# Delta-rule heads of a hybrid encoder layer: spacing, PSUM banks, evictions and tables changed together

## The chip, the core and the metric

The kernel is one launch on one core of a Trainium2 chip. The core has a matrix engine (TensorE, PE in the rows; its weight loads are PEld), VectorE (DVE), ScalarE (ACT), GpSimd (POOL) and a queue that issues transfers (SyncE, SP). The metric is the device time of the launch in microseconds, and lower is better.

## The reference

One encoder layer is applied to 256 prompt tokens and 512 sample tokens (T = 768 together), width 2048, and then normed. The layer projects to 12 groups of columns; a gated delta rule in both directions (8 heads of 128, chunks of 64) and a latent attention (8 heads) run on them; both are gated, projected, mixed and projected again.

```python
proj = rmsnorm(x, norm_in) @ w_in
(qkv, gate_a, a_f, a_b, b_f, b_b, q_lat, kv_lat, k_rope, gate_b, gm_a, gm_b) = split(proj)
qkv = silu(depthwise_conv(qkv)); q_a, k_a = l2norm(q), l2norm(k)      # per head
# gated_delta_chunked, per head and chunk i, forward, and backward on flipped tokens:
a = strict_lower(k_beta @ k.T * decay) + I
u, w = solve_unit_lower(a, [v * beta, k_beta * exp(gc)])
v_new = u - w @ S
o     = (q * exp(g)) @ S + attn @ v_new
S     = S * exp(g_last) + k_dec.T @ v_new
o_a = rmsnorm(o_fwd + o_bwd) * silu(gate_a)
o_b = latent_attention(rmsnorm(q_lat) @ w_q_b, rmsnorm(kv_lat) @ w_kv_b) * silu(gate_b)
m = sigmoid(gm_a) * (o_a @ w_pa) + sigmoid(gm_b) * (o_b @ w_pb)
y = rmsnorm(x + m @ w_out)
```

The kernel puts two chunks of 64 tokens into one tile of 128, so a head has 6 tiles: one sequence of 4 (the sample) and one of 2 (the prompt).

## The kernel before

Products are done in float32 precision from high and low halves, three matmuls each (`project`, L467 on; the weights are cut into halves by `weights`: ScalarE casts `whi`, GpSimd or VectorE subtracts for `wlo`). In time the program has five stages: `w_in` by seven products of half-size blocks (0 to 1236 us); nine more projections of `OTHERS` columns with a sigmoid each, and then the kn, v, qr and qn projections of phase 2 (to 1835); attention beside the `w_pa` projections (to 2110); `w_pb` and `w_out` by seven products again.

The heads of the delta rule (`gdn`, L592 on) are tasks whose matmuls are laid between those of the projections of the second stage. The order on TensorE is the order in which the program is built: every matmul adds its planned cost to `self.clock` (`pin`), a task that yields w comes back when the clock has moved by w, and a matmul is tied to the one before it by a no-sync dependency. `WAIT` is the space between the links of a chain, `STEP` that between pieces of the substitution, `PACE` that between heads. The other engines' order is left to a scheduler, except where `here_on` pins an instruction to the place on its engine at which it was written.

Per head: `gdn_decays` builds E from `rh` (a product of mask and gate, on GpSimd) by two matmuls and an Exp; `gdn_front` transposes k and q, keeps `ktok`, and forms U, the strictly lower blocks; `gdn_values` makes the norms of q and k and `vs`; `gdn_blocks` inverts the 32x32 diagonal blocks by 31 steps of two VectorE operations (L736, L738); `gdn_place` spreads the blocks into X and W, eight copies on ScalarE (L754) and VectorE transposes (L757); `gdn_merge`, one per direction, makes the 64- and 128-wide inverses by 32x32 and 64x64 matmuls; then four chains `gdn_chain` (two sequences, two directions) carry the state S from tile to tile, each tile in three links: S against k and q, r against X (which gives `vn`), `vn` against k and E; `gdn_end` adds the directions, norms, gates and stores the head to `oa_d`.

All small matmuls of the heads and all of attention write to `aps`, tiles of one PSUM bank from a pool of four (`apsum`). In attention the scores of a 128-token block are three matmuls of the 128 unrotated dimensions, one of `qpe` with `kpe[0]` on all 128 rows, and one of `qpe` with `kpe[1]` on 64 rows.

Of the kernel before, what the change touches and what calls it, by code (L numbers as in the profile page):

```python
# [28 lines left out]
WAIT = 2300.0  # L29
STEP = 2500.0  # L30
PACE = 46000.0
# [23 lines left out]
class Layer:  # L55
# [72 lines left out]
    def apsum(self):  # L128
        return self.aux.tile([P, 512], F32, name="aps", tag="a")
# [38 lines left out]
    def work_pools(self):  # L168

        self.les = ExitStack()  # L170
        self.ev = self.pool("ev")
        self.pes = ExitStack()
        self.main = self.pool("main", 2, PSUM, self.pes)
        self.aux = self.pool("aux", 4, PSUM, self.pes)
# [343 lines left out]
    def gates(self):  # L518
# [24 lines left out]
        nc.scalar.activation(u, u, AF.Ln)  # L543
# [14 lines left out]
        nc.scalar.activation(ex, cv, AF.Exp)  # L558
# [20 lines left out]
    def gdn_setup(self):  # L579
        nc, gp = self.nc, self.gp  # L580
        self.X = [gp.tile([P, NCH, P], F32, name=f"X{d}") for d in range(2)]
        self.W = [gp.tile([P, NCH, 64], F32, name=f"W{d}") for d in range(2)]
        for t in self.X + self.W:
            nc.gpsimd.memset(t, 0.0)
# [51 lines left out]
    def gdn_decays(self, s):  # L636
# [3 lines left out]
        for d in range(2):  # L640
            mask = self.minc[d].unsqueeze(1).broadcast_to([P, 3, P])
            for g0 in (0, 3):
                parts = []
                for src in (self.ghi, self.glo):
                    rh = gp.tile([P, 3, P], F32R, name="rh", tag="rh", bufs=3)
                    nc.gpsimd.tensor_tensor(rh, mask, src[:, g0:g0 + 3, d * 8 + h].bitcast(F32).unsqueeze(2).broadcast_to([P, 3, P]), op=ALU.mult)
                    parts.append(rh)
                yield 4000
# [6 lines left out]
        yield 3500  # L655
        s["decayed"] = True

    def gdn_front(self, s):
# [5 lines left out]
        for c0, n, ps in self.tposed(kT):  # L664
            nc.vector.tensor_copy(ktok[:, c0:c0 + n, :], ps)
# [12 lines left out]
        U = s["U"] = gp.tile([P, 2, NCH, P], F32, name="U", bufs=2)  # L678
# [14 lines left out]
    def gdn_values(self, s):  # L693
# [21 lines left out]
    def gdn_blocks(self, s):  # L715
# [3 lines left out]
        U, X, W, V = s["U"], self.X, self.W, self.V  # L719
# [25 lines left out]
    def gdn_place(self, s, R):  # L745

        nc, X, W = self.nc, self.X, self.W
        cols = [R[:, :, 0:24].rearrange("p a (g d n) -> p d n a g", g=2, d=2)[:, d] for d in range(2)]
        for b in range(4):
# [3 lines left out]
            for d, t in zip((1, 0), dst):  # L753
                nc.scalar.copy(t.rearrange("p n (a g) -> p n a g", g=2), cols[d][r])  # L754
# [4 lines left out]
    def gdn_merge(self, s, d):  # L759

        nc, gp, U, X, W = self.nc, self.gp, s["U"][:, d], self.X[d], self.W[d]
# [12 lines left out]
        yield 2600  # L774
# [7 lines left out]
        for p in range(2):  # L782
            A, B = src(p), dst(p)
            nc.vector.tensor_scalar(X[A, :, B], x1[A, :192].rearrange("p (n c) -> p n c", c=32), -1.0, None, op0=ALU.mult)
            if p == d:
                nc.vector.tensor_scalar(W[B, :, wc], x1[B, 192:384].rearrange("p (n c) -> p n c", c=32), -1.0, None, op0=ALU.mult)
        yield 2600
# [5 lines left out]
        nc.vector.tensor_copy(q2s[B], q2[B, :384].rearrange("p (n c) -> p n c", c=64))  # L793
        yield 2600
# [3 lines left out]
        nc.vector.tensor_scalar(X[A, :, B], x2[A, :384].rearrange("p (n c) -> p n c", c=64), -1.0, None, op0=ALU.mult)  # L798
# [6 lines left out]
    def gdn_chain(self, s, q, d):  # L805
# [3 lines left out]
        for step, n in enumerate(chunks):  # L809
# [4 lines left out]
            else:  # L814
                p1 = self.apsum()
                self.mm(p1[:, 0:P], s["kq"][:, 0, ts], S, start=True, stop=True)
                self.mm(p1[:, P:2 * P], s["kq"][:, 1, ts], S, start=True, stop=True)
                r = gp.tile([P, P], F32, name=f"r{q}{d}", tag=f"r{q}{d}")
                nc.vector.scalar_tensor_tensor(r, p1[:, 0:P], self.eg[:, d, n, h:h + 1], s["vs"][:, n, :], op0=ALU.mult, op1=ALU.subtract)
                t = gp.tile([P, P], F32, name=f"t{q}{d}", tag=f"t{q}{d}")  # L820
                nc.scalar.mul(t, p1[:, P:2 * P], self.eg[:, d, n, h:h + 1])
# [9 lines left out]
            p3 = self.apsum()  # L831
# [710 lines left out]
```

## Time and profile before

| what | value |
|---|---|
| time, median of 3 runs (lowest, highest) | 2544.79 us (2543.53, 2544.82) |
| time of the profiled execution | 2548.74 us |
| its span in the profile | 2547.0 us |
| TensorE busy in the span | 2430.3 us (95%) |
| VectorE, ScalarE, GpSimd busy | 1960.1, 1112.6, 539.1 us |

The span runs from the first to the last instruction that the profile shows; 1.74 us of the execution's time lie around it. Busy times are sums of an engine's instructions, overlaps counted once. The rows further down name a tile by the program's name for it, with "out<-in", and a line of the program as L and its number.

### The profile page before, as it was taken

What the parts mean: (1) busy time and instruction counts of PE and PEld (TensorE: products, weight loads), DVE (VectorE), ACT (ScalarE), POOL (GpSimd) and SP (SyncE); (2) the same over time, 40 slices, a digit from 0 to 9 for tenths busy, and PEclk for the clock granted to TensorE, in tenths of its full rate; (3) what the DMA queues carried; (4) which work ended last, traced back from release to release, by engine and by line L of the source; (5) the groups of instructions that cost most, each with busy time, mean ns of one, the idle gap of its engine ahead of it and who ended that gap; (6) DMA issues with size and microseconds to landing.
All of it is one profiled execution on the core that took longest, in us unless ns stands there. A gap on an engine that the chain in (4) does not pass through costs nothing. (4 is left out here: it accounts for less than half of the span.)

```text
span 2547.0 us, 41374 instructions
## 1 busy us (share of the span) xinstructions
PE 2430.3 (95%) x15062; PEld 2303.9 (90%) x15062; DVE 1960.1 (77%) x4294; ACT 1112.6 (44%) x2337; POOL 539.1 (21%) x456
## 2 busy tenths in 40 slices
PE   7999999999999999999989999989999999979997
PEld 6999999999999999999978878878888788968997
DVE  8777888888888887777458899888344567988876
ACT  6553343333333343334526665444344543334442
POOL 5210000000000000000734444443443331032112
PEclk9999999999999999999979999999999999989998
DMA  5542223233222232223312253322375444533346
GB/s 178 180 159 85 102 96 105 97 108 103 97 98 98 96 118 98 98 98 119 125 46 78 77 175 127 119 87 82 114 234 172 137 159 148 176 102 123 130 161 217
DMA packets 157564, 313.45 MB, mean 123 GB/s; under 512 B 17072, under 2 KB 35888, under 8 KB 157360
## 3 DMA queue, kind: packets, MB, share of 16 engines
q1 hardware_dynamic: 157360, 310.81, 36.8%
q8 instruction: 118, 1.93, 0.3%
q14 instruction: 86, 0.70, 0.1%
HBM read 236.33 MB, written 72.45 MB: 121 GB/s over the span
## 5 line engine op out<-in xcount | busy, mean ns | idle before, releaser
L198 ACT CAST Thi<-T 128x512 fp32r<-128x512 f32 x400 | 247.5, 619 | 660.2 <-PE P L86 286.7
L200 DVE TENSOR_TENSOR Tlo<-T,Thi 128x512 fp32r<-128x512 f32 x400 | 284.1, 710 | 225.8 <-ACT Thi L198 221.9
L458 POOL TENSOR_TENSOR wlo<-wraw,whi 128x512 fp32r<-128x512 f32 x113 | 154.3, 1367 | 1179.2 <-ACT whi L453 1124.0
L194 DVE TENSOR_TENSOR T<-wraw,T 128x128 f32<-128x128 f32 x800 | 261.1, 327 | 14.0
L199 DVE TENSOR_TENSOR wlo<-wraw,whi 128x384 fp32r<-128x384 f32 x400 | 227.1, 568 | 0.3 <-ACT whi L191 0.2
L191 ACT CAST whi<-wraw 128x384 fp32r<-128x384 f32 x400 | 203.2, 508 | 39.0 <-PE P L86 31.1
L194 DVE TENSOR_TENSOR T<-wraw 128x256 f32<-128x256 f32 x400 | 169.5, 424 | 9.3 <-DMA wraw<-in_w_pb 6.7
L453 ACT CAST whi<-wraw 128x512 fp32r<-128x512 f32 x130 | 79.9, 617 | 108.5 <-PE ps L86 87.9
L573 DVE SCALAR_TENSOR_TENSOR f<-pad,cols,f 128x772 f32<-128x772 f32 x96 | 97.2, 1012 | 0.1
L736 DVE TENSOR_TENSOR spare<-Y,V 128x126 f32<-128x126 f32 (+22 forms) x248 | 92.0, 371 | 4.8
L738 DVE TENSOR_TENSOR Y<-Y,spare 128x126 f32<-128x126 f32 (+22 forms) x248 | 88.7, 358 | 4.7
L86 PE MATMUL ps<-ch,wlo 128*128 128x512 f32 (+1 forms) x288 | 79.0, 353 | 0.0
L86 PE MATMUL ps<-cl,whi 128*128 128x512 f32 (+1 forms) x288 | 78.7, 351 | 0.0
L86 PE MATMUL ps<-ch,whi 128*128 128x512 f32 (+1 forms) x288 | 78.4, 351 | 0.0
L86 PE MATMUL P<-mS,Thi 128*128 128x384 f32 x224 | 76.4, 343 | 0.7 <-ACT s L230 0.6
L86 PE MATMUL ps<-oah,whi 128*128 128x512 f32 (+1 forms) x256 | 68.4, 345 | 1.6 <-DVE g L1198 1.6
L896 POOL TENSOR_TENSOR acc<-acc,f 128x768 f32<-128x768 f32 x13 | 24.9, 1917 | 206.0 <-DVE wlo L199 131.7
L86 PE MATMUL ps<-oal,whi 128*128 128x512 f32 (+1 forms) x256 | 68.2, 345 | 0.0
L86 PE MATMUL ps<-oah,wlo 128*128 128x512 f32 (+1 forms) x256 | 68.0, 345 | 0.0
L223 DVE TENSOR_TENSOR f<-P,f 128x384 f32<-128x384 f32 x117 | 64.1, 549 | 0.2
L1296 POOL TENSOR_TENSOR rstd<-rstd,x 128x768 f32<-128x768 f32 x13 | 32.8, 2523 | 138.3 <-ACT x L1295 137.9
L1438 POOL TENSOR_TENSOR mX<-R,mH 128x768 fp32r<-128x768 f32 x8 | 30.3, 3782 | 133.0 <-ACT mH L1439 115.5
(779 smaller groups left out, 8158.9 us busy)
## 6 DMA issues: line engine op xcount, KB each, us to landing
wraw<-in_w_in SPq DMA_DIRECT2D x356, 256.0 KB, 2.7
wraw<-in_w_out SPq DMA_DIRECT2D x64, 256.0 KB, 2.7
wraw<-in_w_pa SPq DMA_DIRECT2D x32, 256.0 KB, 3.5
wraw<-in_w_pb SPq DMA_DIRECT2D x32, 256.0 KB, 3.8
xa<-in_xT SPq DMA_DIRECT2D x16, 384.0 KB, 3.7
xtok<-in_x SPq DMA_DIRECT2D x24, 256.0 KB, 3.7
qkv_d<-f SPq DMA_DIRECT2D x24, 256.0 KB, 2.0
sma_d<-f SPq DMA_DIRECT2D x16, 384.0 KB, 2.5
```

Source lines behind the costliest of these rows:

```text
L86: ins = self.nc.tensor.matmul(out, lhsT, rhs, start=start, stop=stop, **kw)
L191: nc.scalar.copy(hi[:, 1:], raw[:, 1:])
L194: tt = lambda o, x, y: self.after_floor(nc.vector.tensor_tensor(o, x, y, op=ALU.add))
L198: nc.scalar.copy(thi, t)
L199: first = nc.vector.tensor_tensor(lo[:, 1:], raw[:, 1:], hi[:, 1:].bitcast(F32), op=ALU.subtract)
L200: last = nc.vector.tensor_tensor(tlo, t, thi.bitcast(F32), op=ALU.subtract)
L223: add = lambda out, a, b, op=ALU.add: nc.vector.tensor_tensor(out, a, b, op=op)
L453: copy = nc.scalar.copy(hi, raw)
L458: eng.tensor_tensor(lo, raw, hi.bitcast(F32), op=ALU.subtract)
L573: nc.vector.scalar_tensor_tensor(acc, pad[:, k:k + 772], w[:, ct, k:k + 1], acc, op0=ALU.mult, op1=ALU.add)
L736: nc.vector.tensor_tensor(tmp[:, :a, :w], Y[:, :a, j:j + 1].broadcast_to([P, a, w]), V[:, j:j + 1, j + 1:].broadcast_to([P, a, w]), op=ALU ...
L738: nc.vector.tensor_tensor(Y[:, :a, j + 1:], Y[:, :a, j + 1:], tmp[:, :a, :w], op=ALU.subtract)
```

## The change

1. **Spaces.** `WAIT` 2300 to 3000, `STEP` 2500 to 2700, `PACE` 46000 to 51000, the spaces inside `gdn_merge` 2600 to 2900, those of `gdn_decays` 4000 to 3000 for head 0 and 9000 for the others.
2. **PSUM.** `aps` has two banks while the heads run. A new pool `link` holds one bank per direction; the two chains of a direction use its two halves. When the heads are done that pool is closed and `aps` gets two more banks.
3. **Inverses.** Two sets of X, taken in turn; a head is placed once the head before the last has finished its chains. U has one buffer instead of two and waits until the head before is merged.
4. **Evictions** of `ktok`, of the merges' X, W and `q2s`, of `vn` and of the first S go from VectorE to ScalarE.
5. **Tables.** The set with both Ln and Exp is loaded once; Sqrt and reciprocal of `gdn_values` and `gdn_end` become Ln, Exp and one Newton step of small GpSimd operations (`inverse_root`); the nine sigmoids of `OTHERS` move to the third stage (`mixed`). The ScalarE copies of `gdn_place` and the Ln of the gates are pinned with `here_on`.
6. **Small moves.** The zeroing of X and W goes from GpSimd to VectorE, and so does `rh` of head 0.
7. **Scores.** The matmul of `qpe` with `kpe[1]` runs on all 128 rows.

```diff
-WAIT = 2300.0
-STEP = 2500.0
-PACE = 46000.0
+WAIT = 3000.0
+STEP = 2700.0
+PACE = 51000.0
...
     def apsum(self):
-        return self.aux.tile([P, 512], F32, name="aps", tag="a")
+        self.aux.append(self.aux.pop(0))
+        return self.aux[-1].tile([P, 512], F32, name="aps", tag="a")
...
-        self.aux = self.pool("aux", 4, PSUM, self.pes)
+        self.cps = ExitStack()
+        self.aux = [self.pool("aux", 2, PSUM, self.pes)]
+        self.link = self.pool("link", 1, PSUM, self.cps)
...
+        both = nc.scalar.preload_act_table_set("natural_log_exp_and_others")
+        self.here_on(both)
...
-        while s["prev"] and not s["prev"].get("chained"):
+        while s["h"] > 1 and not s["prev"]["prev"].get("chained"):
             yield 300
         self.gdn_place(s, R)
...
-                    nc.gpsimd.tensor_tensor(rh, mask, ...)
+                    (nc.gpsimd if h else nc.vector).tensor_tensor(rh, mask, ...)
                     parts.append(rh)
-                yield 4000
+                yield 3000 if h == 0 else 9000
...
-            nc.vector.tensor_copy(ktok[:, c0:c0 + n, :], ps)
+            nc.scalar.copy(ktok[:, c0:c0 + n, :], ps)
...
-        U = s["U"] = gp.tile([P, 2, NCH, P], F32, name="U", bufs=2)
+        while h and s["prev"]["merged"] < 2:
+            yield 500
+        U = s["U"] = gp.tile([P, 2, NCH, P], F32, name="U")
...
-        nc.scalar.activation(sk, ss, AF.Sqrt, bias=self.eps)
-        s["rq"] = small("rq", [NCH])
-        nc.vector.reciprocal(s["rq"], sk[:, 1, :])
+        rr = small("rr", [2, NCH])
+        nc.gpsimd.tensor_scalar(ss, ss, EPS, None, op0=ALU.add)
+        self.inverse_root(rr, ss, sk)
+        s["rq"] = rr[:, 1]
+        nc.gpsimd.tensor_tensor(sk[:, 0], ss[:, 0], rr[:, 0], op=ALU.mult)
...
-                nc.scalar.copy(t.rearrange("p n (a g) -> p n a g", g=2), cols[d][r])
+                self.here_on(nc.scalar.copy(t.rearrange("p n (a g) -> p n a g", g=2), cols[d][r]))
...
-        nc.vector.tensor_copy(q2s[B], q2[B, :384].rearrange("p (n c) -> p n c", c=64))
-        yield 2600
+        nc.scalar.copy(q2s[B], q2[B, :384].rearrange("p (n c) -> p n c", c=64))
+        yield 2900
...
+        bank = self.link.tile([P, 2, 256], F32, name=f"link{d}")
         for q in range(2):
-            self.spawn(self.gdn_chain(s, q, d), WAIT)
+            self.spawn(self.gdn_chain(s, q, d, bank[:, q]), WAIT)
...
-            p2 = self.apsum()
-            self.mm(p2[:, 0:P], self.X[d][:, n, :], r, start=True, stop=True)
+            self.mm(ps[:, 0:P], self.X[h % 2][d][:, n, :], r, start=True, stop=True)
             vn = gp.tile([P, P], F32, name=f"vn{q}{d}", tag=f"r{q}{d}")
-            nc.vector.tensor_scalar(vn, p2[:, 0:P], s["cc" if first else "ncc"][:, d, n:n + 1], None, op0=ALU.mult)
+            nc.scalar.mul(vn, ps[:, 0:P], s["cc" if first else "ncc"][:, d, n:n + 1])
...
+    def inverse_root(self, y, x, t):
+        nc = self.nc
+        nc.scalar.activation(y, x, AF.Ln)
+        nc.scalar.activation(y, y, AF.Exp, scale=-0.5)
+        nc.gpsimd.tensor_tensor(t, y, y, op=ALU.mult)
+        nc.gpsimd.tensor_tensor(t, t, x, op=ALU.mult)
+        nc.gpsimd.tensor_scalar(t, t, -0.5, 1.5, op0=ALU.mult, op1=ALU.add)
+        nc.gpsimd.tensor_tensor(y, y, t, op=ALU.mult)
...
             ps = yield from self.project(KT, self.xs)
             f = self.evt()
             self.scaled(f, ps)
-            nc.scalar.activation(f, f, AF.Sigmoid)
...
-                self.mm(s, qpe[h][:64, qs], kpe[1][:64, keys], start=False, stop=True)
+                self.mm(s, qpe[h][:, qs], kpe[1][:, keys], start=False, stop=True)
...
                 x = raws[j][i]
+                if 72 + j + 8 * i in OTHERS:
+                    nc.scalar.activation(g, g, AF.Sigmoid)
```

Up to the decays of the first head, at the end of the first stage, the order on TensorE is the same in both kernels. The next rows are ScalarE's order, first of before and then of the change, at the placing of head 0 (`spare` holds the inverted blocks, E are decays of later heads, `whi` the weights of the running projection).

```order
L653 ACT_TABLE_LOAD
L653 ACTIVATE E<-aps 128x384
L453 CAST whi<-wraw 128x512
L653 ACTIVATE E<-aps 128x384
L754 COPY X_12973<-spare 32x6x32
L754 COPY W_12974<-spare 32x6x32
L754 COPY X_12973<-spare 32x6x32
L453 CAST whi<-wraw 128x512
L754 COPY W_12974<-spare 32x6x32
L754 COPY X_12973<-spare 32x6x32
```

```order
L661 ACTIVATE E<-aps 128x384
L456 CAST whi<-wraw 128x512 x2
L661 ACTIVATE E<-aps 128x384
L456 CAST whi<-wraw 128x512
L766 COPY X_12977<-spare 32x6x32
L766 COPY W_12980<-spare 32x6x32
L766 COPY X_12977<-spare 32x6x32
L766 COPY W_12980<-spare 32x6x32
L766 COPY X_12977<-spare 32x6x32
L766 COPY W_12980<-spare 32x6x32
```

The table load is gone, three casts of weights stand beside the last two decays' Exp where one stood, and the cast that stood among the copies is behind them. On TensorE 184 matmuls of the projection now stand between the last product of U of head 0 and its first merge (`aps<-W,U`), where 162 stood. The following rows are TensorE's order at the first links of head 0's chains, before and then changed (`vs` against X starts a chain, `ps` are the projection's matmuls; what a row waits for stands in brackets, "Activation" for ScalarE).

```order
L86 MATMUL aps<-vs,X_12973 128x128 [waits DVE_49,Activation_49]
L86 MATMUL aps<-vs,X_12973 128x128 [waits PE_49]
L86 MATMUL aps<-vs,X_12972 128x128 [waits PE_49]
L86 MATMUL aps<-vs,X_12972 128x128 [waits Activation_49]
L86 MATMUL aps<-kq 128x256 [waits DVE_49]
L86 MATMUL aps<-kq 128x256
L86 MATMUL ps<-B5l,whi 128x384 x2
L86 MATMUL ps<-B5h,wlo 128x384 x2
L86 MATMUL ps<-B6h,whi 128x384 x2
L86 MATMUL aps<-vn_13927,kd_13929 128x128 [waits DVE_49]
```

```order
L86 MATMUL link_13869<-vs,X_12977 128x128
L86 MATMUL aps<-rh,mr 128x384 [waits PE_49,Activation_49]
L86 MATMUL aps<-rh,mr 128x384 [waits Pool_49]
L86 MATMUL link_13882<-vs,X_12976 128x128
L86 MATMUL link_13869<-vs,X_12977 128x128 [waits Activation_49]
L86 MATMUL ps<-B5l,whi 128x384 x2
L86 MATMUL ps<-B5h,wlo 128x384
L86 MATMUL link_13882<-vs,X_12976 128x128 [waits Activation_49]
L86 MATMUL ps<-B5h,wlo 128x384
L86 MATMUL ps<-B6h,whi 128x384 x2
L86 MATMUL aps<-kq 128x256 [waits PE_49]
L86 MATMUL link_13869<-vn_13915,kd_13917 128x128 [waits Activation_49]
```

The two sequences of a direction stood side by side, each in a bank of its own; now the second writes to the half beside the first's (`link_13869` twice), and waits until ScalarE has read the first. The last rows are VectorE's order before and ScalarE's now, for the `vn` and S of the same links.

```order
L826 TENSOR_SCALAR vn_13939<-aps,cc 128x128
L826 TENSOR_SCALAR vn_13945<-aps,cc 128x128
L686 SCALAR_TENSOR_TENSOR U<-aps,cc,E 128x128 x4
L729 STREAM_TRANSPOSE PK<-U 32x2x192
L838 COPY S_13969<-aps 128x128
```

```order
L456 CAST whi<-wraw 128x512
L698 COPY qk<-aps 128x256
L838 ACTIVATE vn_13915<-link_13869,cc 128x128
L661 ACTIVATE E<-aps 128x384
L838 ACTIVATE vn_13934<-link_13882,cc 128x128
L838 ACTIVATE vn_13920<-link_13869,cc 128x128
L698 COPY qk<-aps 128x256
L838 ACTIVATE vn_13939<-link_13882,cc 128x128
```

`vn` stood between blocks of U on VectorE, and now stands behind casts of weights and copies of `qk` on ScalarE.

The transposes of the last head's output stand 138 matmuls of projections ahead of the third stage's first one before, and 78 now; the number of projection matmuls from one head to the next is about 187 in both.

## Rows read from the trace of the kernel before

**Rows 1.** The page's first part: busy us, share, instructions.

```profile
PE 2430.3 (95%) x15062; PEld 2303.9 (90%) x15062; DVE 1960.1 (77%) x4294; ACT 1112.6 (44%) x2337; POOL 539.1 (21%) x456
```

**Rows 2.** Windows by stage: length, then busy PE, PEld, DVE, ACT, POOL; granted clock.

```profile
1286.00:1340.00 54.00, 43.49 (x303) 38.12 (x304) 27.40 (x84) 17.84 (x45) 12.34 (x14) 0.65 0.10 33
1340.00:1835.00 495.00, 460.10 (x3736) 407.32 (x3735) 400.31 (x1054) 261.34 (x722) 209.85 (x234) 0.97 0.33 108
1835.00:2110.00 275.00, 274.08 (x1568) 225.55 (x1567) 148.50 (x304) 132.74 (x271) 104.03 (x64) 1.00 0.53 173
2110.00:2547.00 437.00, 389.04 (x2218) 377.64 (x2216) 358.75 (x691) 165.92 (x302) 89.90 (x43) 0.94 0.46 150
```

**Rows 3.** TensorE's waits from 1236 to 1835: us, times, longest.

```profile
PE aps L86 <- POOL rh L646: 9.7, 1, 9.7
PE aps L86 <- ACT t L821: 8.2, 7, 2.2
```

**Rows 4.** Windows of the stretches at half clock: the first, and the sum of all five.

```profile
1295.18:1332.73 37.55, 30.95 (x223) 25.98 (x224) 13.48 (x35) 13.87 (x34) 9.51 (x10) 0.50 0.14 44
...
sum 68.45, PE 60.97 PEld 51.83 DVE 35.64 ACT 25.43 POOL 25.09; mean PE 12.19 PEld 10.37 DVE 7.13 ACT 5.09 POOL 5.02
```

**Rows 5.** Timeline at head 0's placing: start, duration; in brackets idle before, releaser.

```profile
1296.19 0.51 ACT L754 COPY X<-spare 32x192 f32<-32x192 f32 x1 [14.96 <-DVE spare L741]
...
1298.37 1.27 POOL L458 TENSOR_TENSOR wlo<-wraw,whi 128x512 fp32r<-128x512 f32 x1 [14.88 <-ACT whi L453]
...
1300.05 0.46 DVE L757 STREAM_TRANSPOSE W<-spare 32x192 f32<-32x192 f32 x1
...
1300.90 0.83 POOL L646 TENSOR_TENSOR rh<-msk,glo 128x384 fp32r<-128x384 f32 x1
...
1301.78 0.69 PE L86 MATMUL aps<-rh,mr 128*128 128x384 f32 x1 [9.75 <-POOL rh L646]
...
1303.04 1.19 PE L86 MATMUL aps<-W,U 32*32 32x32 f32 x22
```

**Rows 6.** Timeline in head 0's substitution: two operations of one shape, and GpSimd's.

```profile
1279.05 1.42 POOL L458 TENSOR_TENSOR wlo<-wraw,whi 128x512 fp32r<-128x512 f32 x1 [0.48 <-ACT whi L453]
...
1279.36 1.27 DVE L736 TENSOR_TENSOR spare<-Y,V 128x126 f32<-128x126 f32 x1
...
1284.01 0.29 DVE L736 TENSOR_TENSOR spare<-Y,V 128x126 f32<-128x126 f32 x1
```

**Rows 7.** VectorE's groups, 1236 to 1840: costliest and cheapest of the eight moved.

```profile
L826 DVE TENSOR_SCALAR vn<-aps,ncc 128x128 f32<-128x128 f32 x64 | 21.5, 341 | 4.7 <-PE aps L86 4.7
...
L786 DVE TENSOR_SCALAR W<-aps 32x192 f32<-32x192 f32 x16 | 5.6, 353 | 0.3
```

**Rows 8.** ScalarE's groups, 1240 to 1800: busy, mean ns, idle before.

```profile
L821 ACT ACTIVATE t<-aps,ex 128x128 f32<-128x128 f32 x56 | 19.8, 368 | 34.8 <-DVE r L819 34.3 <-POOL E L844 0.3
L653 ACT ACT_TABLE_LOAD x15 | 19.2, 1283 | 0.3
...
L950 ACT ACTIVATE evt<-evt 128x768 f32<-128x768 f32 x8 | 6.8, 845 | 1.5 <-DVE evt L479 1.5
```

**Rows 9.** TensorE's groups by shape, 1835 to 2110: the 64-row matmuls.

```profile
L86 PE MATMUL aps<-L,L 64*128 64x512 f32 x32 | 15.9, 498 | 0.0
...
L86 PE MATMUL aps<-L,L 64*128 64x256 f32 x16 | 6.1, 380 | 0.0
```

**Rows 10.** Timeline of one block of scores; 1905.71 is two matmuls, 128 and 64 rows.

```profile
1905.47 0.40 PE L86 MATMUL aps<-knh,qnl 128*128 128x512 f32 x1
...
1905.71 0.82 PE L86 MATMUL aps<-L,L 128*128 128x512 f32 x2
...
1906.46 0.61 PE L86 MATMUL ps<-oah,wlo 128*128 128x512 f32 x2
```

**Rows 11.** Timeline of SP: the last head's store and the first load behind it.

```profile
1849.31 0.41 SPq L874 DMA_DIRECT2D oa_d<-evt  x1
...
1857.61 0.42 SPq L1179 DMA_DIRECT2D evt<-oa_d  x1
```

More of the change, by code (lines that the diff above doesn't have):

```diff
@@ L542, in gates @@
         nc.vector.tensor_tensor(d, d, r, op=ALU.mult)
-        nc.scalar.activation(u, u, AF.Ln)
+        ln = nc.scalar.activation(u, u, AF.Ln)
+        self.here_on(ln)
         nc.vector.tensor_tensor(u, u, d, op=ALU.subtract)
@@ L557, in gates @@
         ex = c.tile([P, 6, NCH, 8], F32, name="ex")
-        nc.scalar.activation(ex, cv, AF.Exp)
+        both = nc.scalar.preload_act_table_set("natural_log_exp_and_others")
+        self.here_on(both)
+        self.tc.add_manual_dep(both.ins, ln.ins.name, self.nosync, reason="order")
+        self.tables = both.ins.name
+        self.tc.add_manual_dep(nc.scalar.activation(ex, cv, AF.Exp).ins, both.ins.name, self.nosync, reason="order")
         self.eg, self.dec, self.tot = ex[:, 0:2], ex[:, 2:4], ex[:, 4:6]
@@ L580, in gdn_setup @@
         nc, gp = self.nc, self.gp
-        self.X = [gp.tile([P, NCH, P], F32, name=f"X{d}") for d in range(2)]
+        self.X = [[gp.tile([P, NCH, P], F32, name=f"X{i}{d}") for d in range(2)] for i in range(2)]
         self.W = [gp.tile([P, NCH, 64], F32, name=f"W{d}") for d in range(2)]
-        for t in self.X + self.W:
-            nc.gpsimd.memset(t, 0.0)
+        for t in self.X[0] + self.W + self.X[1]:
+            nc.vector.memset(t, 0.0)
         self.V = gp.tile([P, 32, 32], F32, name="V")
@@ L654, in gdn_decays @@
                 nc.gpsimd.tensor_tensor(e, e, mask, op=ALU.mult)
-        yield 3500
+        yield 3500 if h else 1500
         s["decayed"] = True
@@ L718, in gdn_blocks @@
         nc, gp = self.nc, self.gp
-        U, X, W, V = s["U"], self.X, self.W, self.V
+        U, V = s["U"], self.V
         Y = gp.tile([P, 16, 32], F32, name="Y")
@@ L745, in gdn_place @@
     def gdn_place(self, s, R):
-        nc, X, W = self.nc, self.X, self.W
+        nc, X, W = self.nc, self.X[s["h"] % 2], self.W
         cols = [R[:, :, 0:24].rearrange("p a (g d n) -> p d n a g", g=2, d=2)[:, d] for d in range(2)]
@@ L759, in gdn_merge @@
     def gdn_merge(self, s, d):
-        nc, gp, U, X, W = self.nc, self.gp, s["U"][:, d], self.X[d], self.W[d]
+        nc, gp, U, X, W = self.nc, self.gp, s["U"][:, d], self.X[s["h"] % 2][d], self.W[d]
         src = lambda p: slice(64 * p + 32 * d, 64 * p + 32 * d + 32)
@@ L783, in gdn_merge @@
             A, B = src(p), dst(p)
-            nc.vector.tensor_scalar(X[A, :, B], x1[A, :192].rearrange("p (n c) -> p n c", c=32), -1.0, None, op0=ALU.mult)
+            nc.scalar.mul(X[A, :, B], x1[A, :192].rearrange("p (n c) -> p n c", c=32), -1.0)
             if p == d:
-                nc.vector.tensor_scalar(W[B, :, wc], x1[B, 192:384].rearrange("p (n c) -> p n c", c=32), -1.0, None, op0=ALU.mult)
-        yield 2600
+                nc.scalar.mul(W[B, :, wc], x1[B, 192:384].rearrange("p (n c) -> p n c", c=32), -1.0)
+        yield 2900
         A, B = slice(64 * d, 64 * d + 64), slice(64 * (1 - d), 64 * (1 - d) + 64)
@@ L792, in gdn_merge @@
         q2s = s["q2s"]
-        nc.vector.tensor_copy(q2s[B], q2[B, :384].rearrange("p (n c) -> p n c", c=64))
-        yield 2600
+        nc.scalar.copy(q2s[B], q2[B, :384].rearrange("p (n c) -> p n c", c=64))
+        yield 2900
         x2 = self.apsum()
@@ L830, in gdn_chain @@
             yield WAIT
-            p3 = self.apsum()
             if not last:
-                self.mm(p3[:, P:2 * P], kd, vn, start=True, stop=True)
-            self.mm(p3[:, 0:P], s["E"][:, d, n, :], vn, start=True, stop=True)
+                self.mm(ps[:, P:2 * P], kd, vn, start=True, stop=True)
+            self.mm(ps[:, 0:P], s["E"][:, d, n, :], vn, start=True, stop=True)
             if not last:
@@ L837, in gdn_chain @@
                 if first:
-                    nc.vector.tensor_copy(new, p3[:, P:2 * P])
+                    nc.scalar.copy(new, ps[:, P:2 * P])
                 else:
-                    nc.vector.scalar_tensor_tensor(new, S, self.tot[:, d, n, h:h + 1], p3[:, P:2 * P], op0=ALU.mult, op1=ALU.add)
+                    nc.vector.scalar_tensor_tensor(new, S, self.tot[:, d, n, h:h + 1], ps[:, P:2 * P], op0=ALU.mult, op1=ALU.add)
                 S = new
-            nc.scalar.copy(o[:, n, :], p3[:, 0:P])
+            nc.scalar.copy(o[:, n, :], ps[:, 0:P])
             if not first:
@@ L861, in gdn_end @@
             nc.scalar.activation(junk, o[0][:, n, :], AF.Square, scale=rq[:, n:n + 1], accum_out=so[:, n:n + 1])
-        nc.scalar.activation(so, so, AF.Sqrt, bias=self.eps, scale=1.0 / P)
         f = gp.tile([P, NCH], F32, name="f", bufs=2)
-        nc.vector.reciprocal(f, so)
+        nc.gpsimd.tensor_scalar(so, so, 1.0 / P, EPS, op0=ALU.mult, op1=ALU.add)
+        self.inverse_root(f, so, junk[:, :NCH])
         nc.vector.tensor_tensor(f, f, rq, op=ALU.mult)
@@ L1046, in phase2 @@
                 self.les.close()
+                self.cps.close()
+                self.aux.append(self.pool("aux2", 2, PSUM, self.pes))
                 self.wq = self.pool("wq")
```

15 lines of the change are left out of this document (7 added, 8 removed).

## Prediction

> **What bounds the kernel now.** I read the page's busy times first [rows 1]: TensorE is busy for 95% of the span, so a change of the other engines' work pays only where TensorE waits for them or runs slower through it. The windows by stage [rows 2] show where that is. From 1835 to 2110 TensorE is busy for 274.08 of 275 us: nothing but its own work counts there. From 1286 to 1340 it is busy for 43.49 of 54 us at a granted clock of 0.65, and from 1340 to 1835 for 460.10 of 495 at 0.97. Before 1236 the change alters nothing; behind 2110 TensorE's order stays, and its idle time there belongs to the last products.
>
> The waits of TensorE [rows 3] show one large entry in the heads' stage: 9.7 us, once, for `rh` of GpSimd. The next is 8.2 us in seven pieces for `t` of ScalarE, and then shorter lists for `q1s`, `vs`, r and `vn`. A second loss is in the clock: in five stretches the granted clock is 0.50 [rows 4], the lower of TensorE's two levels (1.2 against 2.4 GHz). The first lasts 37.55 us and starts inside the 9.7 us wait; the others have 30.9 us together.
>
> **Term 1, the scores.** Attention has 48 matmuls on 64 rows, 32 of 512 columns and 16 of 256 [rows 9]. Around one of them [rows 10] a 128-row matmul follows its predecessor after 0.24 us (1905.47 to 1905.71), but from 1905.71 to the next at 1906.46, with the 128-row and the 64-row matmul in between, are 0.75 us. Two at 0.24 would be 0.48, so the 64-row one costs 0.27 us more than a full one. The same for all 48 is 13.0 us, and nothing covers it, since TensorE is never idle there [rows 2]. On 128 rows the whole excess should go: −13.0, bounds 0 and −13.0. I take the whole, since all neighbours in the stretch are 128-row matmuls at the short distance.
>
> The Trainium skill bears on this from both sides. Its page "TensorE: Matmul & The Clock Gate", section "Why this matters for your kernels", says that a single matmul on few rows takes the time of a full one; by that alone term 1 is 0. Its page "TensorEngine Tiling (Array Packing)", section "Key Properties", says that a change of tiling mode drains the engine; by that the 0.27 us are two such changes and go away. The trace's 0.75 us speak for the second.
>
> **Term 2, the first head.** The chain is in [rows 5]. ScalarE's queue has a copy of `gdn_place` ahead of a cast of weights, and it waits 14.96 us for the end of the substitution; GpSimd, behind that cast, waits 14.88 us for it, and its next `rh` ends after 1301.7, so TensorE, idle for 9.75 us, goes on at 1301.78. In the window this is 54 − 43.49 = 10.5 us idle [rows 2], and the stretch at half clock makes 30.95 us of work out of 15.5 [rows 4]: 26.0 us in all.
>
> The pinning and the new order on ScalarE put the casts ahead of the copies, so `wlo` and `rh` no longer wait for the substitution. That alone isn't enough: the first merge (1303.04) stands three matmuls behind the stalled one, so TensorE would have come to it at 1293.3 (1303.04 − 9.75), while the last transpose of the placing ends at 1300.5 [rows 5]: 7 us of waiting would stay. Against them stand 22 more matmuls of the projection ahead of the merge (184 − 162, from the order), at three quarters of 0.24 us (384 of 512 columns, [rows 10]) 4.0 us, and a faster substitution: two of its operations of one shape take 1.27 and 0.29 us, the first while GpSimd subtracts [rows 6], and GpSimd's `rh` of the later heads are spread to less than half the rate (yields of 9000 for 4000). Some three such collisions less close the gap. I take −20 of the 26: a rest of 2 us idle and some half clock behind it. Bounds: 0, if the wait only changes its name, and −26.
>
> On the collision the Trainium skill's page "SBUF — State Buffer", section "🔬 SBUF: two separate sides", says that a VectorE operation on two SBUF inputs and a GpSimd operation shut each other out for the whole instruction; the 1.27 against 0.29 us agree, and by it every new small GpSimd operation of `inverse_root` is a cost for the substitution too.
>
> **Term 3, the other heads.** From 1340 to 1835 are 495 − 460.10 = 34.9 us idle [rows 2], and the four later stretches at half clock cost half of 60.97 − 30.95, 15.0 us [rows 4]: 49.9 us at stake. For a gain: a link now has 3000 for 2300 of planned clock ahead of it, and between a head's first and last link I count some 136 projection matmuls where 110 were, 24% more cover for each hand-over; no head waits for the chains of the one before to place its blocks. The eight groups that leave VectorE hold 82 us, from 21.5 down to 5.6 [rows 7], of the 400 that it is busy there. For a loss: ScalarE takes them at about the same price (`t`, the nearest form, 368 ns [rows 8]), and they stand in its queue behind casts and copies; the two sequences of a direction take turns in one bank; `aps` has two banks for four; and U of a head waits for the merge before. ScalarE, busy for 261 of 495 us [rows 2], gains the 82 but sheds about 39 table loads of 1.283 us [rows 8], 50 us (a few fall outside the window), and the sigmoids, 9 × 0.845 [rows 8] = 7.6; so it is not full. GpSimd has some 90 small operations more, for which no row stands; by its shortest in the stage, a 0.31 us memset, 28 us on top of 210, hidden by 285 idle. I take −15, nearly a third of what is at stake, since most of the waits are links that get more cover and a minority get a new hand-over. Bounds: −40 and +20.
>
> **Term 4, the end of the heads.** The last head's output is transposed 78 projection matmuls ahead of the third stage and not 138. 60 matmuls at no more than 0.24 us [rows 10] are up to 14 us; the store, now issued 8.3 us ahead of the first load [rows 11], then comes up to 6 us behind that load's place. The loads of the other seven heads don't depend on it, so part of this is hidden: +3, bounds 0 and +6. The nine sigmoids and their one table load land on ScalarE where it is busy for 166 of 437 us [rows 2]; 9 us there are covered. If they weren't, they would be within the same bounds.
>
> **Sum.** −13.0 − 20 − 15 + 3 = −45.0 against the profiled execution's 2548.74: 2503.7. That execution stands 3.95 us over the median of the runs (2544.79); on their scale the forecast is 2499.8, rounded to 2500.
>
> **Rivals.**
> (a) The scores' rows give nothing, because the excess belongs to the place and not to the rows: term 1 is 0, 2513. Against it, neighbours at 0.24 us in the same block. 8%.
> (b) The first head still stalls: the substitution ends too late, and TensorE stands at `W,U` in place of `rh`. With 5 us idle or more the clock falls as it does in [rows 4]; term 2 is −5, 2515. For it, the 7 us computed above, closed by an estimate. 17%.
> (c) The spaces don't help: the new waits eat what the wider spaces give, term 3 is 0, 2515. 15%.
> (d) Slower. Hand-overs through ScalarE in one bank: both sequences of a direction are under way for two tiles of three links, so 8 heads × 2 directions × 2 tiles × 3 links = 96 times a second matmul waits until ScalarE has read the first's half. The order shows it at the first links (`link_13869` twice, with only three matmuls of other work between). A read takes 0.37 us [rows 8]; with the waits for it before and after, up to 0.5 us: 48 us, and with half clock in the proportion of 15.0 to 34.9 us as in term 3, 69. In place of term 3's −15 this gives 2548.74 − 30 + 69 − 3.95 = 2584. It decides from 30 / (96 × 1.43) = 0.22 us per hand-over on: beyond that the kernel is slower. Against it: behind most of these rows projection matmuls of 0.18 us each stand ahead of the dependent one; I count some 26 waits in the new order with under 0.8 us of TensorE's work since the matmul on which their producer depends, 5 in the old one. 26 at 0.4 us are 10, which is in the bounds of term 3. 7%.
> (e) The spaces do what the counts say, and most of the 49.9 us go: term 3 is −40, 2475. 13%.
>
> **How the numbers follow.** The forecast itself, all four terms near the values taken, has 40%, at 2500 with its own range of 2488 to 2510. The range reaches from 2470, at (e), to 2530, beyond (a), (b) and (c) one by one and two of them together (2528); outside it stay (d) and a little at either end. Under 0.2% (5 us) is about what a measurement can't tell from no change here. Faster is all but (d) and the cases where three things fail: 0.91; the same 0.03, where (d) and the gains cancel; slower 0.06.
>
> **What would show it.** Term 1: no matmul of 64 rows in the third stage, 0.24 us between scores, and the stage from the heads' end to `w_pb` about 13 us shorter at the same busy share. Term 2: no wait near 10 us, copies of `gdn_place` behind the casts, and the stretch at half clock behind the first placing gone or short. If a wait for X or W stands there with over 5 us, it is (b). Term 3: idle time of the heads' stage near 25 us and fewer stretches at half clock; waits for `vn` or S of ScalarE in a sum of 30 us or more are (d). Term 4: a wait for `oah` or `oal` at the head of the third stage. The prediction is wrong if TensorE's idle time in the heads' stage grows, or if the first stage's time moves, which I take as fixed.

## The result and the profile after

The change made the kernel slower. Its median is 2565.99 us (2561.70 to 2566.45, 4 runs) against 2544.81 us of the kernel before in the same comparison: the ratio is 1.0070, 95% interval 1.0053 to 1.0087, some 18 us by the ratio. The forecast was 2500 with a range to 2530. The span of the profiled execution is 2564.1 us, 17.1 longer than before. Of all runs in this document one is set aside as slow, 3895.89 us in e6; the figures of e6 are those of its other nine runs.

The windows of the kernel after, at the same times as [rows 2] (length, busy time of PE, PEld, DVE, ACT and POOL with their instructions, granted clock, DMA share, GB/s):

```profile
1286.00:1340.00 54.00, 50.59 (x379) 45.48 (x378) 25.48 (x64) 27.47 (x89) 21.88 (x29) 0.81 0.15 50
1340.00:1835.00 495.00, 439.22 (x3474) 385.95 (x3473) 338.38 (x799) 262.49 (x834) 208.50 (x289) 0.93 0.31 99
```

The first stretch is better (43.49 to 50.59 us busy, clock 0.65 to 0.81), the second worse (460.10 to 439.22, 0.97 to 0.93). Equal times are not equal work, so I cut both traces at matmuls of the same number of the same kind: one of head 0's projections (the 25th `ps<-S0h,whi`), the first matmul of the third stage (`ps<-oah,whi`), and one behind attention (the 169th of it). First before:

```profile
1236.00:1368.70 132.70, 119.01 (x759) 111.09 (x758) 85.21 (x228) 57.92 (x147) 58.32 (x64) 0.86 0.18 59
1368.70:1871.90 503.20, 470.69 (x3779) 414.76 (x3778) 383.72 (x980) 259.91 (x706) 213.17 (x232) 0.97 0.35 116
1871.90:2073.20 201.30, 200.38 (x1147) 161.53 (x1145) 113.02 (x262) 105.18 (x223) 71.87 (x43) 1.00 0.49 158
```

and then after:

```profile
1236.00:1360.80 124.80, 114.82 (x756) 107.78 (x755) 80.74 (x199) 50.99 (x160) 60.12 (x75) 0.92 0.18 59
1360.80:1902.60 541.80, 489.98 (x3787) 430.07 (x3786) 335.13 (x769) 283.97 (x888) 229.49 (x308) 0.94 0.33 107
1902.60:2088.30 185.70, 183.91 (x1147) 162.33 (x1146) 114.33 (x262) 103.50 (x222) 71.76 (x43) 1.00 0.54 174
```

Head 0 gives 7.9 us, the scores give 15.6, and the heads between them cost 38.6: 503.20 to 541.80. Of these 38.6 half is idle time of TensorE (32.5 to 51.8 us) and half is longer busy time at a lower granted clock (470.69 to 489.98 us for the same matmuls but a few, 0.97 to 0.94). Behind 2088 the two traces differ by 2 us.

What TensorE waits for from 1236 to 1905, after (us in total, times, longest), against [rows 3]:

```profile
PE link L86 <- ACT E L853: 19.1, 13, 2.9
PE link L86 <- ACT t L834: 16.3, 14, 6.0
PE aps L86 <- ACT W L766: 7.5, 4, 3.6
...
PE link L86 <- ACT vn L838: 2.7, 5, 1.0
```

The 9.7 us wait for `rh` is gone. In its place stand two readers of the chains' banks (a bank is one of the pieces of PSUM, the memory that matmuls write to; `link` is such a bank): E, the copy of a tile's output, and t, the old state against q. Neither makes anything that the next link reads. What ScalarE itself waited for, after, from 1236 to 1875:

```profile
ACT t L834 <- DVE r L832: 53.7, 37, 7.7
ACT E L853 <- DVE S L851: 42.8, 24, 5.6
```

One such case from the timeline of the kernel after (start, duration, idle before and releaser):

```profile
1410.30 0.34 DVE L851 SCALAR_TENSOR_TENSOR S<-S,ex,link 128x128 f32<-128x128 f32 x1
...
1410.67 0.27 ACT L853 COPY E<-link 128x128 f32<-128x128 f32 x1 [2.89 <-DVE S L851]
...
1410.99 0.49 PE L86 MATMUL link<-vn,E 128*128 128x128 f32 x2 [2.90 <-ACT E L853]
```

S is read from a bank by VectorE, which had a run of the substitution's operations to do first; E is read from the same bank by ScalarE, after S; and the matmul, whose `vn` had been made 6.4 us earlier, writes to the other half of that bank and so waits for E. Before, that matmul had a bank of its own.

### The profile page after: what moved, and what is told of

The parts are those of the page before. It is cut to its first block, busy times and chain, and to the rows that moved or that the text cites. A ratio compares the mean times of both kernels' runs of the same rounds, so it can differ in the third digit from the quotient of the medians.

```text
span 2564.1 us, 41385 instructions
## 1 busy us (share of the span) xinstructions
PE 2428.3 (95%) x15062; PEld 2312.4 (90%) x15062; DVE 1916.2 (75%) x4068; ACT 1134.2 (44%) x2539; POOL 551.5 (22%) x532
## 4 chain that ended last, share of the span: by engine, by line
PE 73%; DVE 13%; ACT 4%; issue 4%; DMA 3%; POOL 2%; SPq 0%; DVEq 0%; POOLq 0%; ACTq 0%
PE P L86 53%; PE ps L86 12%; PE aps L86 6%; DVE Y L750 3%; DVE spare L748 3%; PE link L86 2%; PE aps L91 1%; DMA xa<-in_xT 1%; DMA wraw<-in_w_out 1%; DVE Tlo L203 0%; DVE T L197 0%; POOL wlo L461 0%; ACT X L766 0%; DVE yT L1413 0%; DVE wlo L202 0%
## 5 line engine op out<-in xcount | busy, mean ns | idle before, releaser
L750 DVE TENSOR_TENSOR Y<-Y,spare 128x126 f32<-128x126 f32 (+22 forms) x248 | 95.9, 387 | 6.8
L1462 POOL TENSOR_TENSOR mX<-R,mH 128x768 fp32r<-128x768 f32 x8 | 30.3, 3785 | 133.4 <-ACT mH L1463 115.7
```

The costliest lines, as they stand in the source:

```text
L750: nc.vector.tensor_tensor(Y[:, :a, j + 1:], Y[:, :a, j + 1:], tmp[:, :a, :w], op=ALU.subtract)
```

## The experiments

Twelve kernels ran. Their times compare by the ratio to the kernel before, each on its own chip; a per cent is 25 us. "Undone" kernels start from the change, "alone" kernels from the kernel before.

| run | kernel | median us | ratio | 95% interval |
|---|---|---|---|---|
| | the change | 2565.99 | 1.0070 | 1.0053 to 1.0087 |
| e1 | change, banks undone | 2534.77 | 0.9966 | 0.9946 to 0.9985 |
| e2 | change, vn and first S on VectorE | 2571.21 | 1.0105 | 1.0086 to 1.0123 |
| e3 | scores alone | 2529.22 | 0.9941 | 0.9921 to 0.9961 |
| e4 | banks alone | 2583.22 | 1.0154 | 1.0134 to 1.0174 |
| e5 | change, old spaces | 2567.28 | 1.0089 | 1.0063 to 1.0115 |
| e6 | banks undone, old spaces | 2550.32 | 1.0033 | 1.0015 to 1.0051 |
| e7 | banks undone, vn and S on VectorE | 2556.15 | 1.0048 | 1.0033 to 1.0064 |
| e8 | scores and pins alone | 2559.35 | 1.0052 | 1.0020 to 1.0084 |
| e9 | banks and pins undone | 2531.86 | 0.9957 | 0.9940 to 0.9975 |
| e10 | scores, spaces, evictions alone | 2528.25 | 0.9937 | 0.9917 to 0.9956 |
| e11 | e10 and the decays | 2520.55 | 0.9895 | 0.9872 to 0.9918 |
| e12 | e9 with one X | 2531.75 | 0.9948 | 0.9928 to 0.9968 |

**Shared banks or ScalarE's queue (e1 to e4).** Theory A: a link in a shared bank waits for readers whose data it doesn't need. Theory B, the rival: the evictions on ScalarE come late in its queue. e1 gives every link a bank of its own again, and with that the other small matmuls (`aps`) four banks instead of two; the rest stays:

```diff
-        self.aux = [self.pool("aux", 2, PSUM, self.pes)]
-        self.link = self.pool("link", 1, PSUM, self.cps)
+        self.aux = self.pool("aux", 4, PSUM, self.pes)
...
+            ps = self.apsum()
             self.mm(ps[:, 0:P], self.X[h % 2][d][:, n, :], r, start=True, stop=True)
```

> The changed kernel with four banks for all small tiles again, so that every link of a chain writes to a bank of its own; all else as changed. Theory A (a link in a shared bank waits until ScalarE has read t and the output out of it, which no data needs): the waits of chain matmuls fall from 44.0 us towards the 22.7 of before, the heads' stage by 20 to 35 us, time 2531 to 2546 us. Theory B (the evictions on ScalarE stand in its queue and come late): less than 8 us change, 2558 to 2574.

2534.77 us: the ratio falls from 1.0070 to 0.9966, 26 us by the ratios and 31 by the medians. In e1's trace, cut at the same matmuls, the heads between head 0 and the third stage take 516.20 us:

```profile
1360.50:1876.70 516.20, 475.05 (x3786) 422.73 (x3785) 333.03 (x767) 278.47 (x888) 226.95 (x308) 0.95 0.35 112
```

So the banks make 25.6 of the 38.6 us; 13.0 stay when every link has its own. e2 moves only two evictions back:

```diff
-            nc.scalar.mul(vn, ps[:, 0:P], s["cc" if first else "ncc"][:, d, n:n + 1])
+            nc.vector.tensor_scalar(vn, ps[:, 0:P], s["cc" if first else "ncc"][:, d, n:n + 1], None, op0=ALU.mult)
...
-                    nc.scalar.copy(new, ps[:, P:2 * P])
+                    nc.vector.tensor_copy(new, ps[:, P:2 * P])
```

> The changed kernel with the evictions of vn and of the first S on VectorE again; banks shared as changed. Theory A: the waits for t and E at the links stay above 30 us, time within 10 us of the changed kernel, 2556 to 2576. Theory B: links wait less, time 2550 or lower.

2571.21 us, within A's range and somewhat slower, not faster. A's "above 30 us" missed: the waits for t and E fell to 20.7 us, and 11.3 us of waits for `vn` on VectorE came in their place. e3 and e4 do one part each on the kernel before:

```diff
-                self.mm(s, qpe[h][:64, qs], kpe[1][:64, keys], start=False, stop=True)
+                self.mm(s, qpe[h][:, qs], kpe[1][:, keys], start=False, stop=True)
```

> The kernel before with only the last matmul of the scores on 128 rows. The offset between the traces shrinks by 15.6 us over the third stage (30.7 to 15.1), so the row edit alone should give 13.0 to 15.6 us: 2529 to 2532. If a matmul on few rows costs what a full one does: 2545.

2529.22 us, 15.0 us by the ratio.

```diff
-        self.aux = self.pool("aux", 4, PSUM, self.pes)
+        self.cps = ExitStack()
+        self.aux = [self.pool("aux", 2, PSUM, self.pes)]
+        self.link = self.pool("link", 1, PSUM, self.cps)
...
+        bank = self.link.tile([P, 2, 256], F32, name=f"link{d}")
         for q in range(2):
-            self.spawn(self.gdn_chain(s, q, d), WAIT)
+            self.spawn(self.gdn_chain(s, q, d, bank[:, q]), WAIT)
...
-            p2 = self.apsum()
+            p2 = bank
```

> The kernel before with only the banks changed: one bank per direction for the chains, two for the rest, two more when the heads are done; evictions, spaces, tables and scores as before. Theory A: chain matmuls wait 15 to 25 us more than the 22.7 of before, time 2560 to 2585. Theory B: within 8 us of before, 2537 to 2553.

2583.22 us, 39 us slower by the ratio, with the evictions on VectorE as before. TensorE's waits in the heads' stage of e4 name the same two readers:

```profile
PE link L86 <- ACT t L825: 10.8, 13, 2.1
PE link L86 <- ACT E L846: 9.3, 11, 3.5
```

B falls and A stands. To see how much of a chain's waits a shared bank makes, I took from each trace every idle time of more than 0.15 us ahead of a chain matmul, and how much of it lay behind the end of the instruction that makes its data (r, S or `vn`; the n-th of a kind in the order is the n-th in the trace). Waits in all, and the part beyond the data: before 17.8 and 8.1 us, after 38.1 and 21.4, e1 32.8 and 6.7, e4 26.6 and 26.4. (The 22.7 and 44.0 us of the expectations are more than the idle times that the traces of before and after list.) So the banks put 13 to 18 us of waits that no data needs on the chains.

Sharing costs more than reuse. In the kernel after, the releaser read the neighbour's half of the bank for 16.9 of the 38.1 us, and all of that lies beyond the data. It read the same chain's half for 19.9, of which only 4.3 lie beyond: there the link's own r or S came from VectorE 0.4 us before the reader was done, on average. With own banks these waits change their name, to r and S (26.4 us in e1, below).

One rival is not separated by a run: e1 and e4 also move the other small matmuls between two banks and four. In e4 two waits of theirs are long, and both releasers only read a bank that the next small matmul writes to:

```profile
PE aps L86 <- ACT aps L670: 8.5, 3, 3.5
PE aps L86 <- DVE vs L715: 7.8, 4, 5.4
```

Outside the chains the small matmuls wait 35.5 us in e4 from 1236 to 1905 against 25.7 before (9.7 of these for `rh`, 1.5 in e4), and 19.1 after against 13.8 in e1. So of what the banks cost, the two banks left for `aps` have a part, about as large as the chains' in e4; how much of the time it is worth was not measured alone.

**The spaces and what else they need (e5 to e8).** e1 still shows 13.8 us of waits for r and 12.6 for S of VectorE:

```profile
PE aps L86 <- DVE r L829: 13.8, 7, 5.9
PE aps L86 <- DVE S L850: 12.6, 7, 2.9
```

So theory C was that the new spaces bring them behind the end of a substitution. e5 is the change and e6 is e1, each with the old three numbers:

```diff
-WAIT = 3000.0
-STEP = 2700.0
-PACE = 51000.0
+WAIT = 2300.0
+STEP = 2500.0
+PACE = 46000.0
```

> The changed kernel with the old WAIT, STEP and PACE (2300, 2500, 46000); banks shared, all else as changed. Theory A (shared banks): the links have less cover for the waits on t and E, so it is slower than the changed kernel's 2566, 2566 to 2590. Theory C (the new spaces bring the state and r of a chain behind the end of the next head's substitution on VectorE, which costs some 10 us): it is faster, 2550 to 2560.

2567.28 us, in A's range; its interval overlaps that of the change.

> The changed kernel with a bank for each link (first run: 2534.8) and with the old WAIT, STEP and PACE. Theory C: the waits for r and S of VectorE, 26.4 us with the new spaces, fall under 15, time 2520 to 2529. If the spaces help as they were taken to in the prediction: slower, 2540 or more.

2550.32 us, 17 us slower than e1 by the ratios. The waits for r and S fell only from 26.4 to 20.3 us, and those for W rose from 8.2 to 16.1. C falls as the main cost of the spaces: with banks of their own they are worth 17 us; with shared banks no difference can be told. e7 is e1 with the same edit as e2.

> The changed kernel with a bank for each link, new spaces, and the evictions of vn and the first S on VectorE. If VectorE's queue is what makes r and S late, 39 us more work on it makes them later: 2540 to 2555. If the move to ScalarE is worth nothing, 2531 to 2539.

2556.15 us, just above the first expectation and 21 us slower than e1: with own banks the two evictions are better on ScalarE.

e8 is e3 with the pins of the placing:

```diff
-                nc.scalar.copy(t.rearrange("p n (a g) -> p n a g", g=2), cols[d][r])
+                self.here_on(nc.scalar.copy(t.rearrange("p n (a g) -> p n a g", g=2), cols[d][r]))
```

> The kernel before with the scores on 128 rows and with the ScalarE copies of the placing pinned; nothing else. On ScalarE two casts of weights and two decays now stand ahead of the first copy. The 9.8 us wait for rh goes; TensorE stands at the first merge instead for up to 7 us, and part of the half clock behind it stays. From the 2529.2 of the scores alone: 2515 to 2525. If the wait only changes its name: 2527 to 2531.

2559.35 us against 2529.22: the pins alone cost 28 us by the ratios, outside both expectations. The timeline of e8 at head 0:

```profile
1301.29 0.84 ACT L950 ACTIVATE evt<-evt 128x768 f32<-128x768 f32 x1 [15.88 <-DVE evt L479]
...
1303.83 0.50 ACT L754 COPY X<-spare 32x192 f32<-32x192 f32 x1
...
1304.80 0.84 PE L86 MATMUL aps<-W,U 32*32 32x32 f32 x12 [9.02 <-ACT W L754]
```

The copies now stand behind a sigmoid that waits 15.88 us for VectorE, and TensorE stands 9.02 us at the first merge instead of 9.75 us at `rh`. But the 28 us are not lost here. Cut at the same matmuls, e8 is:

```profile
1236.00:1361.90 125.90, 110.89 (x763) 104.98 (x762) 86.72 (x227) 58.60 (x149) 59.90 (x67) 0.93 0.19 63
1361.90:1893.20 531.30, 490.78 (x3780) 430.67 (x3779) 382.68 (x981) 255.16 (x702) 210.48 (x231) 0.93 0.34 109
```

e3 has 133.5 and 502.9 us there: head 0 is 7.6 us shorter with the pins, and the later heads are 28.4 longer. In them TensorE waits 17.1 us for W, against 1.1 in e3, and its granted clock is 0.93 against 0.97. A pin holds an instruction back to its place; it doesn't bring it forward.

**What is left of the other parts (e9 to e12).** e9 takes the pins of the copies out of e1; e10 adds to e3 the spaces (not those of the decays) and the evictions of part 4; e11 adds to e10 the decays' spaces (with the last of head 0's, 3500 to 1500, which the list of the change leaves out) and the `rh` of head 0; e12 takes the second X and the wait of U out of e9. Their edits, cut short, in this order:

```diff
-                self.here_on(nc.scalar.copy(t.rearrange("p n (a g) -> p n a g", g=2), cols[d][r]))
+                nc.scalar.copy(t.rearrange("p n (a g) -> p n a g", g=2), cols[d][r])
```

```diff
-WAIT = 2300.0
-STEP = 2500.0
-PACE = 46000.0
+WAIT = 3000.0
+STEP = 2700.0
+PACE = 51000.0
...
-                    nc.vector.tensor_copy(new, p3[:, P:2 * P])
+                    nc.scalar.copy(new, p3[:, P:2 * P])
```

```diff
-                yield 4000
+                yield 3000 if h == 0 else 9000
```

```diff
-        while s["h"] > 1 and not s["prev"]["prev"].get("chained"):
+        while s["prev"] and not s["prev"].get("chained"):
```

> The changed kernel with a bank for each link (2534.8) and without the pins on the ScalarE copies of the placing. If the pins hold the copies back, as the 27.1 us of waits for W with the pins alone show, the 8.2 us of waits for W shrink and it takes 2520 to 2531. If the pins are what removed the 9.8 us wait for rh, that wait is back: 2538 to 2550.

2531.86 us, just above the first expectation. The waits for W fell from 8.2 to 3.5 us, and head 0 is past its mark 15.8 us earlier than in the kernel before (e1: 8.3). At the third stage it is only 4.7 us ahead of the kernel before: most of that gain is lost over the later heads. By the ratios e9 is 2 us better than e1, inside the intervals.

> The kernel before with the scores on 128 rows (2529.2), the new spaces (those of the decays excepted) and all evictions of part 4 on ScalarE; old banks, tables, one set of X, no pins. If spaces and evictions gain without the other parts what they gained where they were undone (18 and 21 us): 2495 to 2515. If they gain only because X has two sets and the tables are gone: 2524 to 2540.

2528.25 us, the same as e3. So the 17 and 21 us that are lost when spaces and evictions are undone in e1 don't show as gains over the kernel before.

> The kernel of the run before the last (old banks, tables, one X, no pins; scores, spaces, evictions new; 2528) with the new spaces of the decays and the rh of head 0 on VectorE. There TensorE waited 9.8 us for rh of head 0 and some 21 us at later rh for a bank that t still held. If decays that are spread wider meet fewer such banks and the first wait goes: 2500 to 2518. If the waits move to the first merge and to other tiles: 2524 to 2535.

2520.55 us, ratio 0.9895: 1.05% faster than the kernel before, the best version found, between its two expectations. The 9.8 us wait for `rh` is gone, and the waits for t are 12.6 us where e10 had 21.6:

```profile
PE aps L86 <- ACT t L821: 12.6, 7, 3.1
```

> The changed kernel with own banks and without pins (2531.9), and with one set of X and two buffers of U as before. If a second X lets the placing come early and spares waits: slower, 2536 to 2550. If the early placing is what puts r and S of the chains behind it on VectorE (27.6 us of waits): 2515 to 2527.

2531.75 us, between its two expectations; the intervals of e9 and e12 overlap, so the second X buys nothing that can be measured here. The waits for r and S fell from 27.6 to 8.3 us with one X, but those for t rose from 7.1 to 16.4 and 5.6 for E came.

## Why the prediction was wrong

**Term 1, the scores, was right.** −13.0 was forecast; the cut traces give −15.6 and e3 −15.0 alone. The timeline of the kernel after, at one block of scores:

```profile
1921.35 0.39 PE L86 MATMUL aps<-knh,qnl 128*128 128x512 f32 x1
1921.58 0.62 PE L86 MATMUL aps<-L,L 128*128 128x512 f32 x2
1922.04 0.51 PE L86 MATMUL ps<-oah,whi 128*128 128x512 f32 x2
```

The pair that took 0.75 us in [rows 10] takes 0.46. The excess of 0.29 us is of one size with the 0.27 of the forecast; 48 of them are 13.9. Of the two rules of the Trainium skill that stood against each other, the one of "TensorEngine Tiling (Array Packing)", section "Key Properties", that a change of mode drains the engine, agrees with the trace. The sentence of the Trainium skill's page "TensorE: Matmul & The Clock Gate", section "Why this matters for your kernels", on a single matmul doesn't hold for one between full ones: here it cost 0.29 us more. That the excess is a drain is not shown by a run, only that it goes with the 64 rows.

**Term 2, the first head, was mis-sized: its gap was to be closed by a faster substitution, which did not come.** −20 was forecast, −7.9 came. The wait for `rh` went, and TensorE stood at `W,U` in its place, as rival (b) says, though for 1.40 and 1.33 us and not 5. The timeline of the kernel after:

```profile
1287.61 1.29 POOL L461 TENSOR_TENSOR wlo<-wraw,whi 128x512 fp32r<-128x512 f32 x1
1287.77 1.20 DVE L748 TENSOR_TENSOR spare<-Y,V 128x56 f32<-128x56 f32 x1
...
1289.00 0.22 DVE L750 TENSOR_TENSOR Y<-Y,spare 128x56 f32<-128x56 f32 x1
...
1291.38 0.51 ACT L766 COPY X<-spare 32x192 f32<-32x192 f32 x1 [4.93 <-DVE spare L753]
...
1292.36 0.56 PE L86 MATMUL aps<-W,U 32*32 32x32 f32 x12 [1.40 <-ACT W L766]
...
1294.25 0.84 PE L86 MATMUL aps<-W,U 32*32 32x32 f32 x12 [1.33 <-ACT W L766]
```

The first copy starts at the end of the substitution, so nothing in ScalarE's queue held it back here. The substitution began 5.1 us earlier than before but was no faster: 31.7 us from its first operation to its last, where before it took 31.4. The prediction let "some three such collisions less" close the gap; GpSimd was busy beside it for 17.3 us, and for 16.6 before. The pins have a part in that. e1 and e9 differ in them alone: with them three casts of weights stand between 1270 us and the copies, GpSimd's subtractions behind these casts run beside the substitution (17.1 us of GpSimd), and it takes 30.3 us; without them one cast stands there, it is 11.9 us of GpSimd, and it takes 26.6.

The stretch at half clock behind the placing, in a window as in [rows 4]:

```profile
1293.53:1314.01 20.48, 19.76 (x161) 17.55 (x162) 1.97 (x4) 8.64 (x29) 4.68 (x5) 0.50 0.20 67
```

It makes 19.76 us of busy time out of 9.9, a loss of 9.9 us where 15.5 stood and where the forecast left about 4. Without the pins (e9) the head gives 15.8. The prediction took the pinning for the cure. e8 shows that pins alone change the name of the wait, and e11, which has none, that the spread decays and the `rh` on VectorE are enough to remove it. The wait is not all that head 0's time hangs on: in e10 it stands at 9.8 us, and the mark comes 15.0 us earlier all the same, with 10.2 us at half clock. (With the new spaces some of the heads' small matmuls move behind the mark, 738 matmuls ahead of it for 759, so these 15.0 are not quite for equal work.)

**Term 3, the other heads, is the step that failed.** −15 was forecast and +38.6 came; the sign was wrong. Of the 38.6, 25.6 go with the banks (e1). The prediction saw that mechanism as rival (d), hand-overs in one bank, gave it 7% and set it aside by a count: 26 waits with little of TensorE's work ahead of them, at 0.4 us each, "in the bounds of term 3". For `aps` with two banks it had no price at all. Two things were wrong in setting it aside.

- The price. A hand-over was priced as ScalarE's read, 0.37 us and a little. The trace shows 27 waits of the links for E and t with 35.4 us (19.1 and 16.3), 1.3 us each, because the reader itself waits for VectorE's read of the same bank: E for S, t for r, 42.8 and 53.7 us in all. VectorE has its substitution to do, and S and r stand behind several of its operations at times. Of the 35.4 us, 19.8 lie beyond the data; in the rest r or S itself was late.
- The count. It followed each link to the matmul that its data comes from. The waits that came run through another instruction: a reader of an old value, most of all in the neighbour's half. An order shows such a wait as one more semaphore, but not that its releaser stands behind another engine's queue.

Half of the +38.6, 19.3 us, is longer busy time, at a granted clock of 0.94 for 0.97. Rival (d) took half clock in the proportion of term 3 and forecast 2584 in all; the neighbour's half held TensorE 19 times and not 96, for 0.9 us each where 0.5 was priced, and the measured 2566 lies below it. The sign named for (d), 30 us of waits for `vn` or S of ScalarE, did not come (2.7 us for `vn`): the readers were E and t. The gain for which term 3 counted, more cover by wider spaces, is there only beside own banks (e6 against e1, 17 us; e5 against the change, none) and nothing over the kernel before can be told by itself (e10 against e3).

That ScalarE's read waits for VectorE's (by a semaphore of the program), though both only read, was in the rows of before as well (`t` idle for 34.3 us behind r [rows 8]); I read it as ScalarE's idle time, which costs nothing, and missed that the change makes TensorE wait for it. The Trainium skill, "PSUM — Partial Sum Buffer", section "Terms", says that two engines must not touch one bank at once, reads against reads included; by that the two reads are always in a row. The 37 waits for r, 53.7 us, agree.

**Term 4, the end of the heads,** was +3 within 0 to +6. No wait for `oah` or `oal` stands in the list after, and the offset of the traces is 30.7 us at the end of the projections ahead and 30.7 at the first matmul of the third stage: 0.

The terms as measured, −15.6 − 7.9 + 38.6 + 0 and 2 behind, make the 17 us between the spans. What would have shown the prediction wrong, idle time of TensorE that grows in the heads' stage, is what came.

**What stays open.** Where the 13.0 us of the later heads come from that stay in e1, how the banks' cost divides between the shared `link` and the two banks of `aps`, why the gain at head 0 in e9 is lost again over the later heads, and why e1 has later r and S on VectorE than the kernel before although VectorE has less to do, was not taken apart. Each edit moves the whole order on VectorE and ScalarE, and runs of one kernel lie up to 17 us apart (e9, 2524.69 to 2541.49).

## What to carry to other kernels

When a tile of PSUM is reused or shared, list its readers, not only the producer of the next matmul's data: each reader becomes a gate, with all that is queued ahead of it and ahead of any other engine that reads the bank first. Here a neighbour's reader cost most, since nothing of the waiting matmul's own data was due. A dependency that only holds back (a pin) removes no wait; ask what stands ahead of the pinned instruction in its queue. Gains that show when parts are undone one by one need not add up from the other side: two of these parts are worth 17 and 21 us inside one combination, and together nothing that can be told outside it.

## What the runs showed of the hardware

A matmul on 64 rows of contraction between full ones cost 0.29 us more than a full one of the same 512 columns. An operation of the substitution on 56 elements took 1.20 us on VectorE beside a subtraction on GpSimd, and the next one on 56 elements 0.22 us without it; in [rows 6] it is 1.27 and 0.29 us for one shape. Behind waits of only 1.40 and 1.33 us at head 0, between small 32x32 matmuls, TensorE ran at the lower clock (0.50) for 20.48 us.
